# State-space stage of a hybrid decoder block: constant operand rows and the memory tokens' norm and splits made in the convolution stage and loaded; the exp table loaded behind attention

## The chip, the cores and the metric

One Trainium2 chip, of which one core runs this program. The core has a matrix engine (PE, with its weight loads listed apart as PEld), a vector engine (DVE), a scalar engine (ACT), a general engine (POOL) and a queue that issues DMA transfers (SP). The metric is the time of one execution on the device in microseconds; less is better.

## What is computed

One layer of a decoder trunk on 1024 tokens of width 1024, in three sub-layers, each with a norm before and after it and a residual. The change touches the first two:

```python
h = rms_norm(x, g_pre_mix)
q, k, v, z, xbc, dt_raw, ga, gs = split(h @ w_in)
o_att = stick_breaking_attention(q, k, v)                 # 16 heads of 64
o_ssm = ssd_branch(z, xbc, dt_raw, ...)                   # 32 heads in 4 groups, chunks of 128
merged = sigmoid(ga) * (o_att @ w_br_att) + sigmoid(gs) * (o_ssm @ w_br_ssm)
x = x + rms_norm(merged @ w_mix_out, g_post_mix)
h = rms_norm(x, g_pre_xa)
mem_n = rms_norm(mem, g_mem)                              # 256 memory tokens
x = x + rms_norm(memory_cross_attention(h, mem_n, w_xq, w_xkv, w_xo), g_post_xa)
...                                                       # dense SwiGLU
```

Inside `ssd_branch`, `x|B|C` go through a causal convolution of four taps and a SiLU. Then, for each chunk of 128 tokens, with `a_cs` the running sum of `dt * a` in the chunk:

```python
decay  = exp(where(tril, a_cs[l] - a_cs[s], -inf))        # per head, 128 x 128
y_diag = (C B^T * decay) (x dt)
states = B^T (decay_to_end * x dt)                        # passed from chunk to chunk
y_off  = exp(a_cs) * (C states_before)
```

## The kernel before

The program is one straight list of instructions without loops on the chip. A scheduler orders them at compile time, engine by engine: nearly as they are written, with later work moved up where it reckons an engine free and a buffer of the pool available. Buffers with one tag share a fixed number of slots. `behind(marks)` and `issue_behind` hold instructions behind a given one of the same engine. A float32 product is made as three products of split operands: `hi` is the rounded part, `lo` the rest (`hi_sb`, `lo_of`, `mm3`, L85 to L103).

Stages in order of time: the pre-norm; the token-major projections; the **convolution stage** (L476 to L615); **attention** (L625 to L828), with the last gates' projections (`gate_proj`, L711) between the heads; the **state-space stage** (L838 to L1180); the merge (L1197); cross-attention; the feed-forward layer.

*Convolution stage.* 18 pairs of 128 columns of `w_in` go through `pair` (L523): twelve with `conv`, six with `gate`. Each pair makes seven weight combinations on POOL (L198 to L201), splits them on ACT and DVE (L94, L97) into nine slots `sw`, multiplies (84 matmuls, L229 to L231), and adds up on DVE (L246 to L250). `conv` has three multiply-adds on DVE (L509), a sigmoid on ACT (L510) and a product on POOL (L511); its result is stored, or turned by PE transposes in `tail` (L499) during the next pair. Results and temporaries of 4 KB a partition share the six slots `b4`. Two small chains are set between the pairs: `dt_chain` (L540) ahead of the seventh, `dt_columns` (L587) ahead of the ninth.

*State-space stage.* The decay matrices come from a matmul (L937) of two operands whose rows hold a constant pattern and some rows of data: `colrows` (two buffers of 128 x 1024) gets rows of `sum_d` per chunk (L930), `keyrows` (two of 128 x 512) gets rows of `key_d` per four chunks (L894). The patterns are filled and selected on POOL (L874 to L879) and copied and completed on DVE (L882 to L886). All of the stage is then run over 32 chunks: `prep` two chunks ahead (loads, decay matmul, exp on ACT at L938, splits), `states`, `outp` (the matmuls `pd` at L989, the gated norm), and `flip` (four PE transposes of the chunk's output, L1011), which is called two chunks behind. `open_four` (L888) loads `bfm`, `cfm`, `btm` per four chunks; each of the three has a single buffer.

*Memory tokens.* `memory(m)` (L1058) loads 128 memory tokens, squares and norms them with the gain `gm`, turns them by eight PE transposes (L1067) and splits them into `mh`, `mlo` (L1069, L1070). It is called for both halves behind the first two `prep`. `mem_quanta` (L1072) then projects the tokens to keys and values in small pieces that are set between the first chunks' steps, and loads its own weights (L1083).

The exp table of ACT is loaded by the first exp of the stage, at L938; attention uses sigmoids (L714, L749) and copies.

The input `h` of the projections is held in eight tiles (b11, b21, b22, t1) on the left side of the memory up to the last gate projection. What the state-space stage allocates there takes their place; in order, these are the accumulators (L833), then `gbs`, `smp`, `s4p`, `s2p`, `exps`, `wr3`. The operand rows lie in `exps`.

## Time and profile before

| | |
|---|---|
| median of 3 runs | 2601.34 us (2600.95 to 2601.63) |
| the profiled execution's own time | 2600.91 us |
| its span in the trace | 2599.2 us |
| PE busy in the span | 2499.2 us (96%) |
| DVE busy | 1785.8 us (69%) |
| ACT busy | 1143.2 us (44%) |
| POOL busy | 864.8 us (33%) |
| convolution stage, first and last L229 on b11 | 287.7 to 627.5 us |
| attention's last matmul (L777) | 1109.8 us |
| decay matmuls (L937), first and last | 1117.7 to 1425.3 us |

Times are from one profiled execution and count from the start of its span. An engine's busy time says little by itself; what counts is which wait ends last at a given place. A view that lists stretches gives the busy time of each engine in each of them, and the TensorE clock that was granted, as a share of full speed.

### The profile page before, as it was taken

The page shows a single profiled execution, that of the slowest core. Times are in us where ns is not written, and L with a number is a line of the kernel's source. Part 1 is how long each engine was busy: PE and PEld are TensorE (multiplying, and loading weights), DVE is VectorE, ACT ScalarE, POOL GpSimd, SP SyncE. Part 2 cuts the span into 40 slices and gives each one's busy share as a digit, 9 for nine tenths or more (in the row PEclk, how much of TensorE's full clock was granted, in tenths as well). Part 3 has the DMA queues.
Part 4 walks back from the last instruction along what each step waited for, and adds up shares of the span by engine and source line. Part 5 has one row for each costly group of instructions (what it writes and reads, how often), then busy time and mean ns, then how long its engine had stood idle before and what let it go on. Part 6 is the DMA issues. An engine that isn't in the chain of part 4 may idle for free. (4 is left out here: it accounts for less than half of the span.)

```text
span 2599.2 us, 32676 instructions
## 1 busy us (share of the span) xinstructions
PE 2499.2 (96%) x12026; PEld 2072.4 (80%) x12026; DVE 1785.8 (69%) x2082; ACT 1143.2 (44%) x2037; POOL 864.8 (33%) x664
## 2 busy tenths in 40 slices
PE   5999999999999999989999999999999999999998
PEld 4888887788788888878888787887787888887876
DVE  7446778776477777588888665415459666665997
ACT  5333455555465665556544312314333333334343
POOL 5212544443211222235655150101114333323762
PEclk8999999999999999989999999999999999999999
DMA  5331343333534343356332472311232222234232
GB/s 176 111 108 57 122 130 101 106 113 114 154 98 110 92 124 93 91 177 196 107 95 71 142 251 84 119 61 49 81 118 73 78 90 81 77 93 170 98 130 98
DMA packets 250666, 288.50 MB, mean 111 GB/s; under 512 B 16767, under 2 KB 173064, under 8 KB 250122
## 3 DMA queue, kind: packets, MB, share of 16 engines
q1 hardware_dynamic: 250506, 286.41, 35.3%
q8 instruction: 95, 1.56, 0.2%
q14 instruction: 65, 0.53, 0.1%
HBM read 196.56 MB, written 73.01 MB: 104 GB/s over the span
## 5 line engine op out<-in xcount | busy, mean ns | idle before, releaser
L750 DVE TENSOR_TENSOR_SCAN n<-n,mask 128x128 f32<-128x128 f32 (+7 forms) x128 | 180.4, 1434 | 23.5 <-ACT n L749 22.2
L97 DVE TENSOR_TENSOR sw<-sf,sw 128x512 fp32r<-128x512 f32 x150 | 128.8, 871 | 67.5 <-ACT sw L94 67.2
L198 POOL TENSOR_TENSOR sf<-wr,wr 128x512 f32<-128x512 f32 x38 | 57.0, 1499 | 275.4 <-DMA wr<-in_w_in_dram 108.3
L767 ACT ACTIVATE wth<-tr,mone 128x512 fp32r<-128x512 f32 x192 | 109.9, 583 | 80.0 <-PE tr L764 79.3
L94 ACT ACTIVATE sw<-sf 128x512 fp32r<-128x512 f32 x150 | 92.0, 626 | 110.8 <-PE mm L231 95.1
L768 DVE SCALAR_TENSOR_TENSOR wtl<-tr,wth 128x512 fp32r<-128x512 f32 x192 | 99.4, 544 | 55.2 <-ACT wth L767 55.2
L94 ACT ACTIVATE sw<-wr 128x512 fp32r<-128x512 f32 x113 | 71.0, 629 | 127.2 <-PE mm L231 127.0
L231 PE MATMUL mm<-h,sw 128*128 128x512 f32 x320 | 124.8, 391 | 1.8 <-DVE sw L97 1.8
L100 PE MATMUL mm<-oth,bw 128*128 128x512 f32 (+1 forms) x320 | 122.3, 382 | 3.4 <-DVE a L1048 2.3
L229 PE MATMUL mm<-h,sw 128*128 128x512 f32 x320 | 122.6, 391 | 2.9 <-ACT h L94 2.3
L230 PE MATMUL mm<-h,sw 128*128 128x512 f32 x320 | 125.1, 391 | 0.0
L97 DVE TENSOR_TENSOR sw<-wr,sw 128x512 fp32r<-128x512 f32 x113 | 103.7, 918 | 24.8 <-ACT sw L94 16.9
L102 PE MATMUL mm<-oth,bw 128*128 128x512 f32 (+1 forms) x320 | 119.6, 374 | 0.6 <-DVE bw L97 0.6
L101 PE MATMUL mm<-otl,bw 128*128 128x512 f32 (+1 forms) x320 | 119.0, 372 | 0.0
L97 DVE TENSOR_TENSOR zl<-zr,zh 128x512 fp32r<-128x512 f32 x84 | 67.6, 810 | 72.3 <-ACT zh L94 72.1
L509 DVE SCALAR_TENSOR_TENSOR b<-b,prmT,b 128x1023 f32<-128x1023 f32 (+2 forms) x72 | 108.0, 1500 | 13.3 <-ACT b L507 12.7
L90 POOL TENSOR_SCALAR v<-va 128x512 fp32r<-128x512 f32 x16 | 20.6, 1288 | 277.3 <-PE av L777 164.6
L167 POOL TENSOR_SCALAR rstd<-ms 128x1 f32<-128x1 f32 x74 | 29.4, 397 | 238.8 <-ACT x L1269 113.0
L749 ACT ACTIVATE n<-sc 128x512 f32<-128x512 f32 (+1 forms) x192 | 88.6, 493 | 45.7 <-PE tr L764 28.9
L100 PE MATMUL p<-bw,h 128*128 128x512 f32 x256 | 99.6, 394 | 3.3 <-DVE x L1271 2.4
L94 ACT ACTIVATE zh<-zr 128x512 fp32r<-128x512 f32 x84 | 52.4, 630 | 113.8 <-PE mb L415 55.4
L102 PE MATMUL p<-bw,h 128*128 128x512 f32 x256 | 100.6, 394 | 0.0
(587 smaller groups left out, 8163.7 us busy)
## 6 DMA issues: line engine op xcount, KB each, us to landing
wr<-in_w_gu_dram SPq DMA_DIRECT2D x80, 256.0 KB
wr<-in_w_in_dram SPq DMA_DIRECT2D x36, 512.0 KB
zr<-in_w_in_dram SPq DMA_DIRECT2D x24, 512.0 KB
gu_d<-t SPq DMA_DIRECT2D x44, 256.0 KB
wraw<-in_w_in_dram SPq DMA_DIRECT2D x20, 512.0 KB
x<-in_x_dram SPq DMA_DIRECT2D x16, 512.0 KB
zs_d<-zo SPq DMA_DIRECT2D x32, 256.0 KB
xs_d<-b SPq DMA_DIRECT2D x32, 256.0 KB
```

The lines of the kernel that those rows point to most:

```text
L94: A.activation(o, i, AF.Copy)
L97: eng.tensor_tensor(o, i, hi.bitcast(F32), ALU.subtract)
L100: first = T.matmul(ps, sh, mh, start=start, stop=False)
L101: T.matmul(ps, sh, ml, start=False, stop=False)
L102: T.matmul(ps, sl, mh, start=False, stop=stop)
L229: T.matmul(ps, w[0][:, k, :], b[0][:, k, :], start=first and k == 0, stop=False, skip_group_check=True)
L230: T.matmul(ps, w[0][:, k, :], b[1][:, k, :], start=False, stop=False, skip_group_check=True)
L231: T.matmul(ps, w[1][:, k, :], b[0][:, k, :], start=False, stop=last and k == 3, skip_group_check=True)
L509: V.scalar_tensor_tensor(acc[:, sh:], y[:, :S - sh], cw(3 - sh, f), acc[:, sh:], ALU.mult, ALU.add)
L750: V.tensor_tensor_scan(nt[:, 0:L][:, ::-1], nt[:, 0:L][:, ::-1], mask[:, S - L:][:, ::-1], 1.0, ALU.mult, ALU.max)
L767: A.activation(wh[:, t0 * P:], pt[:, t0 * P:], AF.Identity, bias=mone)
L768: V.scalar_tensor_tensor(wl[:, t0 * P:], pt[:, t0 * P:], -1.0, wh[:, t0 * P:].bitcast(F32), ALU.add, ALU.subtract)
```

## The change

1. `patterns()`, called ahead of the second pair of the convolution stage, makes one copy of each operand-row pattern in slots `b4` and stores them to `colpat_d` and `keypat_d`. In the state-space stage, four loads fill the two `colrows` and the two `keyrows`. The pool `exps` is allocated first in its stage.
2. `memory()`, called ahead of the third pair, norms, turns and splits the memory tokens there, in slots `b4` and `b2` and the stage's own PSUM buffers, and stores the two parts to `mem_d`. In the state-space stage, four loads fill `mh` and `mlo`.
3. A one-column exp behind the last gate's sigmoid (`warm`).
4. The transposes of a chunk's `flip` are held behind the last `pd` matmul of the chunk two further on.
5. `FILL_LEFT`, an unused stretch of memory, shrinks by the 32 bytes that `warm` takes.

```diff
-FILL_LEFT, FILL_RIGHT = 128, 224
+FILL_LEFT, FILL_RIGHT = 96, 224
...
+    colpat_d = scr("colpat_d", [P, S])
+    keypat_d = scr("keypat_d", [P, HALF])
+    mem_d = [scr(f"mem_d{i}", [P, KT, ML]) for i in range(2)]
...
+            def patterns():
+                col, row, t = [mk(t4, [P, S], F32, "b4") for _ in range(3)]
+                before = t.rearrange("p (h s) -> p h s", s=P)
+                G.memset(before, 1.0)
+                G.affine_select(before, before, [[0, GH], [-1, P]], ALU.is_gt, 0.0, base=-2 * PAIRS, channel_multiplier=2)
+                V.tensor_copy(col.bitcast(F32R), t)
...
+                V.tensor_tensor(col[hr].rearrange("p (h s) -> p h s", s=P).bitcast(F32R), *heads, ALU.add)
+                nc.sync.dma_start(colpat_d, col)
+                within = row[:, HALF:].rearrange("p (c s) -> p c s", s=P)
+                G.memset(within, -(2.0 ** 120))
...
+                V.tensor_copy(row[:, 0:HALF].bitcast(F32R), row[:, HALF:])
+                V.tensor_scalar(row[ONES:ONES + 2, 0:HALF].bitcast(F32R), ident[ONES:ONES + 2, 0:1].to_broadcast([2, HALF]), 0.0, 1.0, ALU.mult, ALU.add)
+                nc.sync.dma_start(keypat_d, row[:, 0:HALF])
+
+            def memory():
+                gm, junk = [mk(t4, [P, D], F32, "b4") for _ in range(2)]
+                nc.sync.dma_start(gm, a["g_mem"][0].partition_broadcast(P))
+                for m in range(2):
+                    xt = mk(t4, [P, D], F32, "b4")
+                    nc.sync.dma_start(xt, a["mem"][0][m * P:(m + 1) * P, :])
+                    ms = mk(stats, [P, 1], F32, "ms")
+                    A.activation(junk, xt, AF.Square, scale=D ** -0.5, accum_out=ms)
+                    V.scalar_tensor_tensor(xt, xt, rstd_of(ms), gm, ALU.mult, ALU.mult)
+                    for kh in range(2):
+                        pt = mk(ps1, [P, HALF], F32, "tr")
+                        for k in range(4):
+                            T.transpose(pt[:, k * P:(k + 1) * P], xt[:, (kh * 4 + k) * P:(kh * 4 + k + 1) * P], ident)
+                        hi, lo = [mk(t2, [P, HALF], F32, "b2") for _ in range(2)]
+                        A.activation(hi.bitcast(F32R), pt, AF.Copy)
+                        V.tensor_tensor(lo.bitcast(F32R), pt, hi, ALU.subtract)
+                        for d, t in zip(mem_d, (hi, lo)):
+                            nc.sync.dma_start(d[:, kh * 4:kh * 4 + 4, m * P:(m + 1) * P], t.rearrange("p (k t) -> p k t", t=P))
+
             for i, j in enumerate(order):
+                if i == 1:
+                    patterns()
+                if i == 2:
+                    memory()
                 if i == 6:
                     dt_chain()
...
-                    A.activation(gt, ps, AF.Sigmoid)
+                    gated.append(A.activation(gt, ps, AF.Sigmoid))
...
+            with behind(gated[-1:]):
+                A.activation(warm, mone, AF.Exp)
...
+        ep = pool(p3, "exps", 1)
         gb = pool(p3, "gbs", 2)
         sm = pool(p3, "smp", 2)
         t4 = pool(p3, "s4p", 3)
         t2 = pool(p3, "s2p", 9)
-        ep = pool(p3, "exps", 1)
...
         for t in colrows:
-            V.tensor_copy(t, before)
-            V.tensor_tensor(t[hr], ...)
+            nc.sync.dma_start(t.rearrange("p h s -> p (h s)").bitcast(F32), colpat_d)
         for t in keyrows:
-            V.tensor_copy(t.rearrange("p (c s) -> p c s", s=P), within)
-            V.tensor_scalar(t[ONES:ONES + 2], ...)
+            nc.sync.dma_start(t.bitcast(F32), keypat_d)
...
-            for k in range(4):
-                T.transpose(pt[:, k, :], y[:, k * P:(k + 1) * P], ident)
+            with behind([chk[n + 2]["last"]] if n + 2 in chk else []):
+                for k in range(4):
+                    T.transpose(pt[:, k, :], y[:, k * P:(k + 1) * P], ident)
...
-        for m in range(2):
-            memory(m)
+        for kh in range(2):
+            for t, src in zip((mh, mlo), mem_d):
+                nc.sync.dma_start(t[:, kh * 4:kh * 4 + 4].bitcast(F32), src[:, kh * 4:kh * 4 + 4])
```

The old `memory(m)` and its tiles `gj`, `gm`, `junk_m` are gone from the state-space stage, as are the POOL fills and selects of L874 to L879.

More of the change, by code (lines that the diff above doesn't have):

```diff
@@ L155, in hybrid_block @@
     G.memset(mone, -1.0)
+    warm = mk(cp, [P, 1], F32, "warm")
     stats = pool(ctx, "stats", 16)
@@ L252, in winograd_pair @@
         return pa_
+    NROW, HEADS, ONES, PAIRS, LARGE = 2, 32, 0, 64, 2.0 ** 127
     HB = ("b11", "b21", "b22", "t1")
@@ L709, in qk_proj @@
                 return dense(C_Q + hp * P, ev_q), dense(C_K + hp * P, ev_k)
+            gated = []
             def gate_proj(gi):
@@ L859, in hybrid_block @@
         four = {}
-        NROW, HEADS, ONES, PAIRS, LARGE = 2, 32, 0, 64, 2.0 ** 127
         low = mk(ep, [P, P], F32, "low")
@@ L872, in hybrid_block @@
         keyrows = [mk(ep, [P, HALF], F32R, f"keyrows{i}") for i in range(2)]
-        before, within = mk(t4, [P, GH, P], F32, "s4"), mk(t4, [P, GH, P], F32, "s4")
-        G.memset(before, 1.0)
-        G.affine_select(before, before, [[0, GH], [-1, P]], ALU.is_gt, 0.0, base=-2 * PAIRS, channel_multiplier=2)
-        within = within[:, 0:4]
-        G.memset(within, -(2.0 ** 120))
-        G.affine_select(within, within, [[0, 4], [1, P]], ALU.is_ge, 0.0, base=2 * PAIRS, channel_multiplier=-2)
-        G.affine_select(within, within, [[0, 4], [-1, P]], ALU.is_ge, 0.0, base=1 - 2 * PAIRS, channel_multiplier=2)
-        hr = slice(HEADS, HEADS + 2 * GH)
         for t in colrows:
-            V.tensor_copy(t, before)
-            V.tensor_tensor(t[hr], *[ident[hr, HEADS + j * GH:HEADS + (j + 1) * GH].unsqueeze(2).to_broadcast([2 * GH, GH, P]) for j in range(2)], ALU.add)
+            nc.sync.dma_start(t.rearrange("p h s -> p (h s)").bitcast(F32), colpat_d)
         for t in keyrows:
-            V.tensor_copy(t.rearrange("p (c s) -> p c s", s=P), within)
-            V.tensor_scalar(t[ONES:ONES + 2], low[ONES:ONES + 2, 0:1].to_broadcast([2, HALF]), 0.0, 1.0, ALU.mult, ALU.add)
+            nc.sync.dma_start(t.bitcast(F32), keypat_d)
         def open_four(g, q):
@@ L991, in outp @@
                     marks.append(ins)
+            d["last"] = ins
             V.tensor_tensor(y, y, pd, ALU.add)
@@ L1052, in hybrid_block @@
         mlo = mk(ot, [P, KT, ML], F32R, "otl")
-        gj = mk(wp, [P, 4, D], F32, "bw")
-        gm, junk_m = gj[:, 0], gj[:, 1]
-        nc.sync.dma_start(gm, a["g_mem"][0].partition_broadcast(P))
         marks = []
-        def memory(m):
-            xt = mk(wr, [P, D], F32, "wraw")
-            nc.sync.dma_start(xt, a["mem"][0][m * P:(m + 1) * P, :])
-            ms = mk(stats, [P, 1], F32, "ms")
-            A.activation(junk_m, xt, AF.Square, scale=D ** -0.5, accum_out=ms)
-            V.scalar_tensor_tensor(xt, xt, rstd_of(ms), gm, ALU.mult, ALU.mult)
-            for kh in range(2):
-                pt = mk(ps, [P, 4, P], F32, "mm", bufs=2)
-                for k in range(4):
-                    T.transpose(pt[:, k, :], xt[:, (kh * 4 + k) * P:(kh * 4 + k + 1) * P], ident)
-                ks, cs = slice(kh * 4, kh * 4 + 4), slice(m * P, (m + 1) * P)
-                A.activation(mh[:, ks, cs], pt, AF.Copy)
-                V.tensor_tensor(mlo[:, ks, cs], pt, mh[:, ks, cs].bitcast(F32), ALU.subtract)
         def mem_quanta():
```

4 lines of the change are left out of this document (added).

## Prediction

> **What bounds the kernel now.** I began with the page: the profiled execution has a span of 2599.2 us, 1.7 us less than its own time of 2600.91 us, and PE is busy nearly everywhere in it.
>
> ```profile
> span 2599.2 us, 32676 instructions
> ```
>
> The change touches two places only: the convolution stage (L476 to L615) and the seam at which attention ends and the state-space stage begins. So I next read the table of stretches around the seam (columns: stretch, its length, then busy us and instructions of PE, PEld, DVE, ACT, POOL, then the granted clock, the DMA share and GB/s).
>
> ```profile
> 1100.00:1110.00 10.00, 7.45 (x41) 5.22 (x39) 5.39 (x11) 5.63 (x11) 1.48 (x3) 1.00 0.56 150
> 1110.00:1120.00 10.00, 6.28 (x19) 3.85 (x18) 9.17 (x15) 6.67 (x11) 2.99 (x4) 0.52 0.68 207
> 1120.00:1130.00 10.00, 9.91 (x50) 8.24 (x50) 10.00 (x9) 8.45 (x16) 7.70 (x6) 0.80 0.72 216
> 1130.00:1140.00 10.00, 6.94 (x29) 4.79 (x29) 10.00 (x13) 5.43 (x9) 2.09 (x3) 0.71 0.50 145
> 1140.00:1150.00 10.00, 10.00 (x65) 9.81 (x66) 8.26 (x11) 4.17 (x9) 5.51 (x7) 0.78 0.44 130
> ```
>
> Two losses of PE are to be seen. It is idle for 2.55 + 3.72 + 0.09 + 3.06 = 9.4 us, and what it does run from 1110 on runs at a lowered clock: busy time times the missing share gives 6.28 x 0.48 + 9.91 x 0.20 + 6.94 x 0.29 + 10.00 x 0.22 = 9.2 us (an estimate, since the clock is a mean of its stretch). Together 18.6 us are lost here. DVE is busy 9.17 + 10.00 + 10.00 = 29.2 of the 30 us from 1110 to 1140, so between these points it is DVE that PE waits for, directly or through a chain.
>
> The timeline of the seam shows what stands in these queues (start, us, engine, line, operation; in brackets the idle time before it and its releaser).
>
> ```profile
> 1102.16 0.60 ACT L714 ACTIVATE gt<-mm 128x512 f32<-128x512 f32 x1 [0.24 <-PE mm L102]
> 1102.31 0.42 SPq L898 DMA_DIRECT2D cfm<-cf_d  x1
> 1103.26 6.68 SPq L900 DMA_DIRECT2D btm<-bt_d  x2
> ...
> 1106.79 0.63 ACT L94 ACTIVATE ch<-cfm 128x512 fp32r<-128x512 f32 x1 [2.37 <-DMA cfm<-cf_d]
> ...
> 1107.94 0.44 PE L776 MATMUL av<-wth,v 128*128 128x384 f32 x1 [2.07 <-ACT wth L767]
> ...
> 1109.66 1.28 DVE L882 CAST colrows<-s 128x1024 fp32r<-128x1024 f32 x2
> 1110.86 0.76 DVE L885 CAST keyrows<-s 128x512 fp32r<-128x512 f32 x2
> 1111.65 2.35 DVE L883 TENSOR_TENSOR colrows<-ident 16x1024 fp32r<-16x1024 f32 x2
> 1113.09 4.30 SPq L930 DMA_DIRECT2D colrows<-sum_d  x4
> 1115.82 0.41 DVE L886 TENSOR_SCALAR keyrows<-low 2x512 fp32r<-2x512 f32 x1
> ...
> 1117.65 1.19 PE L937 MATMUL dec<-colrows,keyrows 128*128 128x512 f32 x2 [1.37 <-DMA colrows<-sum_d]
> 1117.96 1.28 ACT L938 ACT_TABLE_LOAD   x1
> ```
>
> The chain to the first decay matrix is: last attention step, constants on DVE, the rows of `sum_d` written into them, matmul at 1117.65, exp table, exp. A different wait comes earlier: ACT stands 2.37 us for `cfm` with the last attention copies behind it in its queue, and PE's 2.07 us before L776 come from that.
>
> **The change, part by part.** *Constants.* From DVE's seam go 1.28 + 0.76 + 2.35 + 2 x 0.41 = 5.2 us. In their place stand four loads, 2 x 512 KB + 2 x 256 KB. Their tiles move to the front of the pool, so to addresses which the projections' input h held; they come free when the last gate projection is done, about 1102, not behind the last attention step. The `sum_d` and `key_d` rows now wait for these loads, where they waited for DVE. Behind them on SP stand the `btm`, `xs` and memory loads. The other bound on this is SP itself: for 6.68 us from 1103.26 it is held by the second `btm`, which waits for its only buffer, so `sum_d` may still not go out before about 1110, 3 us earlier than now.
>
> *Memory tokens.* The norm, the transposes and the splits leave the seam.
>
> ```profile
> L1063 DVE SCALAR_TENSOR_TENSOR wraw<-wraw,rstd,bw x2: 1693/1874/2056, 1119.4 to 1126.3; 128x1024 f32<-128x1024 f32 x2
> L1070 DVE TENSOR_TENSOR otl<-mm,oth x4: 674/676/677, 1129.9 to 1140.4; 128x512 fp32r<-128x512 f32 x4
> 1123.12 1.46 PE L1067 MATMUL mm<-ident,wraw 128*128 128x128 f32 x8
> 1130.63 1.25 PE L1067 MATMUL mm<-ident,wraw 128*128 128x128 f32 x8 [0.72 <-DVE otl L1070]
> 1610.24 1.03 PE L180 MATMUL tr<-ident,x 128*128 128x128 f32 x8
> ```
>
> That is 2 x 1.87 + 4 x 0.68 = 6.5 us of DVE, and 2.7 us of PE, which at full clock would be 2 x 1.03 = 2.1 us (eight such transposes at L180). With the constants DVE loses 11.7 of its 29.2 us in the bound stretch. The split tokens come back as four loads of 512 KB in place of the gain and the two token loads of 512 KB each, and their first user, the memory projection, which started only behind L1070's last at 1140.4, can fill PE's hole at 1130 to 1140.
>
> *DMA at the seam.* 1.5 MB of constants and 2 MB of tokens come, 1.5 MB go: 2.0 MB more, on five more issues. From 1100 to 1130 the rows move 1.50 + 2.07 + 2.16 = 5.7 MB; 7.8 MB would need 27 us at the 293 GB/s of the next row (PE, clock, DMA share, GB/s). They fit, but not by much, and if they don't, 1.5 MB cost 5.4 us.
>
> ```profile
> 640.00:645.00 5.00, 5.00 (x24) 1.00 0.96 293
> ```
>
> *Exp table.* The load of 1.28 us goes from between the first decay matmul and its exp to behind the last gate's sigmoid, which ran at 1102.16. There the 2.37 us that ACT stands before `ch` cover it; without that cover it would delay the last attention copies by 1.3 us. The Trainium skill ("ScalarE: Activation LUTs", What ACT_TABLE_LOAD costs) counts about 2.66 us for a switch, a drain included; by that the term would be 2.7 us and not 1.3. The row shows 1.28 us alone, the exps following at once, so the sum goes by 1.3.
>
> *Seam, summed.* Of the 9.4 us of idle time I keep the tail of attention (2.55, its cause `cfm` is untouched) and half of 3.72, as `sum_d` gains 3 us at best and the table 1.3; the hole of 3.06 I take as filled but for 0.5. That gives 1.9 + 2.5 = 4.4. Of the clock's 9.2 I keep half, 4.6, as the first gap stays and with it the first lowering. The transposes give 2.1 at full clock. Sum 11.1; I take **10 us**, since DVE can also be late with what it has left. Lower bound 3 us (only `sum_d`'s lead, everything else waiting for loads), upper 17 (all but the tail's idle time and two clock us).
>
> *Convolution stage.* All of it is added there: POOL work, one set of constants on DVE (half of 5.2), the memory tokens' 6.5, so 9.1 us of DVE, ACT's squares and copies, 16 transposes, some 4.3 MB on 13 issues of SP.
>
> ```profile
> 290.00:310.00 20.00, 19.25 (x85) 15.58 (x84) 15.73 (x18) 9.57 (x16) 11.99 (x9) 1.00 0.53 158
> 310.00:330.00 20.00, 20.00 (x94) 16.64 (x93) 18.84 (x16) 10.21 (x17) 11.76 (x8) 1.00 0.30 92
> 330.00:350.00 20.00, 20.00 (x94) 16.64 (x93) 13.41 (x14) 11.37 (x17) 9.36 (x6) 1.00 0.46 153
> 350.00:370.00 20.00, 20.00 (x94) 16.66 (x93) 14.51 (x13) 10.01 (x16) 10.03 (x6) 1.00 0.38 112
> ...
> 430.00:450.00 20.00, 16.06 (x66) 12.11 (x64) 19.79 (x27) 8.03 (x10) 8.97 (x6) 0.91 0.19 56
> 450.00:470.00 20.00, 18.87 (x87) 15.43 (x88) 13.95 (x22) 12.46 (x21) 6.27 (x4) 1.00 0.53 158
> ```
>
> PE is full there, so the transposes cost their 2.1 us in any case. DVE's 9.1 us meet 4.3 + 1.2 + 6.6 + 5.5 = 17.6 us of idle time in 80, ACT has half its time free, and 4.3 MB fit beside 92 to 158 GB/s. So stalls can be zero. The other bound is the place where such work was already put in, `dt_chain` (L540): from 430 to 470 DVE fills up to 19.79 of 20, and PE loses 3.94 + 1.13 of idle time and 16.06 x 0.09 = 1.4 of clock, 6.5 us. With DVE at 18.84 (310 to 330) PE still lost nothing, so I take a value in the lower half, 2 us. **Cost 4 us**, bounds 2 and 9.
>
> The squares need no table of their own there: in the last stage, too, squares (L1698) run behind sigmoids (L1436) without a load between them.
>
> *Order of the flips.* Holding a flip's transposes behind the last `pd` matmul two chunks on is what PE does anyway, chunk for chunk, so I cost it at nothing (at most 0.6 us each in the first chunks).
>
> ```profile
> 1310.30 1.89 PE L989 MATMUL pd<-s,s 128*128 128x96 f32 x16
> 1314.86 0.60 PE L1011 MATMUL ptr<-ident,s 128*128 128x128 f32 x4
> ```
>
> **Sum.** 2600.9 - 10 + 4 = 2594.9; the profiled execution is 0.4 us under the median of 2601.34, so 2595 is the time either way. A measurement of this kernel can tell about 0.2%, 5.2 us, from no change.
>
> **Rivals.** *Loads take DVE's place*: SP's queue holds the constants' rows up to 1110 and the tokens land no sooner than the projection began. The seam then gives its lower bound, 3 to 5, the stage takes 4: 2601. For it speaks the 6.68 us row; against it that DVE's 29.2 of 30 us lose 11.7 whatever SP does.
>
> *The convolution stage takes it back*: stalls as at `dt_chain`, 6.5, with 2.1 of transposes, 8.6 in all, and 10 at the seam: 2599. What would make it so are POOL's new fills and selects, as DVE slows beside POOL:
>
> ```profile
> 310.18 2.27 POOL L201 TENSOR_TENSOR sf<-wr,sf 128x512 f32<-128x512 f32 x1
> 311.23 1.78 DVE L97 TENSOR_TENSOR sw<-sf,sw 128x512 fp32r<-128x512 f32 x1
> 316.42 0.68 DVE L97 TENSOR_TENSOR sw<-sf,sw 128x512 fp32r<-128x512 f32 x1
> ```
>
> The same subtraction takes 0.68 us alone and 1.78 beside L201. The Trainium skill says as much ("GPSIMD Engine Reference", 1. Specifications): the SBUF interfaces are shared, with contention for DVE instructions of two SBUF inputs. The trace agrees, by 1.1 us in this pair.
>
> *Slower*: the constants' 1.5 MB go out ahead of `cfm`. Then `cfm` lands 5.4 us later, ACT holds the last attention copies behind `ch`, and the whole seam shifts by that; it decides itself by SP's order at 1102 and by ACT keeping `ch` ahead of L767. Of the 10 us then 10 - 5.4 - 1.9 (the tail's gap, 2.07, more than doubled, brings an earlier clock loss) = 3 are left, and with stalls of 9 in a stage that gets its weights through the same SP queue behind the tokens' stores: +6, 2607.
>
> *More*: the projection fills all of PE's holes, the clock stays up: 16 at the seam, 3 in the stage, 2588.
>
> *It doesn't do what it says*: a sigmoid scheduled behind the early table load would bring the load back at 1.28 us, in the seam: part of the first rival.
>
> **Chances.** Forecast 0.42 (own range 2591 to 2598; three quarters of it beyond 5.2 us), more 0.15, loads 0.15, convolution 0.13, slower 0.15. Faster by over 0.2%: 0.33 + 0.15 = 0.48; within: 0.09 + 0.15 + 0.13 = 0.37; slower 0.15. The range of 8 in 10 is 2586 to 2606: it leaves out the better part of "more" and half of "slower".
>
> **What would show it.** DVE from 1110 to 1140 well under 29 us; the first L937 at about 1113 to 1115, no table load before its exp; the memory projection's first matmuls before 1135; PE's clock above 0.9 after 1130; in the stage PE full from 290 to 370 but for 4 us, its end (last L231 there) 4 us later than now. I am wrong if `cfm`, the constants or the tokens release PE at the seam, or if PE shows gaps of 2 us and a lowered clock before 400.

## The result: 17.9 us slower, and the profile after

The changed kernel took 2619.34 us (median of 4 runs, 2618.66 to 2623.62), the kernel before, run beside it, 2601.49 us (2600.95 to 2603.95). The ratio is 1.0068, with a 95% interval of 1.0055 to 1.0081: slower by 0.7%, where 0.2% can be told from no change. The forecast was 2595 us.

The profiled execution of the changed kernel took 2618.99 us. Its page begins so:

```profile
span 2617.2 us, 32721 instructions
```

Three groups of matmuls cut the span into stages: the scores (`sc`, attention), `av` (their product with the values) and `pd` (the output of each chunk of the state-space stage). The view of a tile's instructions gives each group's first start and last end (columns: line, engine, operation, count; ns min, median, max; first and last start or end in us; forms). First the kernel before:

```profile
L747 PE MATMUL sc<-kh,qs x192: 218/389/504, 691.8 to 1088.5; 128*128 128x512 f32 x96, 128*128 128x128 f32 x32, 128*128 128x256 f32 x32, 128*128 128x384 f32 x32
L748 PE MATMUL sc<-kl,qs x192: 220/364/479, 692.9 to 1088.8; 128*128 128x512 f32 x96, 128*128 128x128 f32 x32, 128*128 128x256 f32 x32, 128*128 128x384 f32 x32
L989 PE MATMUL pd<-s,s x512: 243/275/421, 1124.9 to 1448.2; 128*128 128x96 f32 x149, 128*128 128x64 f32 x22
```

Then the changed kernel:

```profile
L804 PE MATMUL sc<-kh,qs x192: 218/389/501, 705.8 to 1105.4; 128*128 128x512 f32 x96, 128*128 128x128 f32 x32, 128*128 128x256 f32 x32, 128*128 128x384 f32 x32
L805 PE MATMUL sc<-kl,qs x192: 223/364/475, 707.0 to 1105.6; 128*128 128x512 f32 x96, 128*128 128x128 f32 x32, 128*128 128x256 f32 x32, 128*128 128x384 f32 x32
L1032 PE MATMUL pd<-s,s x512: 242/275/423, 1135.3 to 1465.0; 128*128 128x96 f32 x149, 128*128 128x64 f32 x22
```

| stretch | before | after | difference |
|---|---|---|---|
| start to first `sc` (convolution stage and what lies ahead of it) | 691.8 | 705.8 | +14.0 |
| first to last `sc` (attention) | 397.0 | 399.8 | +2.8 |
| last `sc` to last `pd` (seam and state-space stage) | 359.4 | 359.4 | 0.0 |
| last `pd` to the end | 1151.0 | 1152.2 | +1.2 |
| span | 2599.2 | 2617.2 | +18.0 |

So the seam, forecast to give 10 us, gave nothing, and the convolution stage, forecast to cost 4, cost 14. The last line is within what that stretch, which the change doesn't touch, differs by among the kernels below (1149 to 1156 us). The 2.8 us of attention stay unexplained: the kernels with an edit in the convolution stage have 397.6 to 400.4 there, those without 397.0 to 398.9.

**The seam.** The table of stretches of the changed kernel, 16 us later than the rows of the prediction, since attention ends 15.6 us later (columns as there):

```profile
1116.00:1126.00 10.00, 8.39 (x46) 6.11 (x43) 4.64 (x8) 6.85 (x13) 0.50 (x2) 1.00 0.70 221
1126.00:1136.00 10.00, 7.33 (x20) 4.84 (x21) 5.17 (x7) 5.69 (x10) 1.28 (x2) 0.57 0.90 284
1136.00:1146.00 10.00, 9.14 (x48) 8.19 (x48) 6.47 (x6) 4.31 (x8) 4.62 (x4) 0.75 0.83 274
1146.00:1156.00 10.00, 10.00 (x79) 9.60 (x80) 10.00 (x11) 4.97 (x9) 4.34 (x3) 1.00 0.92 279
1156.00:1166.00 10.00, 8.84 (x66) 8.18 (x65) 8.44 (x9) 7.04 (x13) 8.50 (x8) 1.00 0.90 269
```

DVE was busy 29.2 of 30 us there and is busy 5.17 + 6.47 + 10.00 = 21.6 now: that relief came. What took its place is the DMA: 0.83 to 0.92 busy for 40 us at 269 to 284 GB/s, where before it was 0.44 to 0.72. The timeline just behind attention's last matmul:

```profile
1125.40 0.33 PE L834 MATMUL av<-wtl,v 128*128 128x128 f32 x1
...
1127.85 2.04 PE L955 MATMUL dec<-cfm,bfm 128*128 128x128 f32 x8 [2.11 <-DMA cfm<-cf_d]
...
1129.88 2.24 PE L980 MATMUL dec<-colrows,keyrows 128*128 128x512 f32 x3
...
1131.06 1.04 POOL L987 TENSOR_TENSOR s<-s,wm 128x512 f32<-128x512 f32 x1 [11.45 <-DMA s<-xs_d]
```

The first decay matmul comes 4.5 us behind the last `av`, not 7.9. But PE now waits for `cfm`, and POOL's product of `xs` and `wm` (L987) waits for the load of `xs`. In the kernel before, POOL had done that work ahead of attention's end at 1109.8 (POOL's timeline):

```profile
1089.27 0.95 POOL L874 MEMSET s<- 128x1024 f32 x1 [22.56 <-PE sc L748]
...
1093.57 1.04 POOL L944 TENSOR_TENSOR s<-s,wm 128x512 f32<-128x512 f32 x1
1094.57 0.63 POOL L879 TENSOR_SCALAR_AFFINE_SELECT s<-s 128x512 f32<-128x512 f32 x1
1095.17 2.49 POOL L944 TENSOR_TENSOR s<-s,wm 128x512 f32<-128x512 f32 x2
1097.63 1.49 POOL L978 TENSOR_TENSOR s<-s,dsk 128x512 f32<-128x512 f32 x1
```

The constants are gone from there, as meant, but so are four products of L944 (the fourth at 1100.01) and one of L978: `exps` stands first among the pools now, the tiles of `xs` lie behind it, and come free with attention's last tiles. (That this place is the reason is tested in e8, below.)

In these five rows the loss of PE (the stretch less busy time times clock) falls from the 18.6 us of the prediction to 1.6 + 2.7 + 0.9 + 0 + 1.2 = 6.3 of idle time and 7.33 x 0.43 + 9.14 x 0.25 = 5.4 of clock, 11.7 in all: 6.9 less.

How much of the relief stayed? Two rows per kernel, cut at the last `av` matmul: its first 60 us and the next 80. Before:

```profile
1109.80:1169.80 60.00, 52.50 (x318) 45.78 (x319) 50.88 (x58) 36.06 (x62) 24.22 (x24) 0.80 0.59 180
1169.80:1249.80 80.00, 77.31 (x422) 65.25 (x421) 64.16 (x72) 46.99 (x86) 42.84 (x38) 1.00 0.55 176
```

After:

```profile
1125.40:1185.40 60.00, 53.36 (x332) 46.73 (x332) 47.91 (x48) 33.88 (x59) 31.94 (x24) 0.89 0.78 244
1185.40:1265.40 80.00, 73.15 (x382) 60.25 (x381) 65.14 (x73) 45.20 (x83) 43.70 (x39) 0.98 0.50 165
```

In the first 60 us the loss falls from 60 - 52.50 x 0.80 = 18.0 to 60 - 53.36 x 0.89 = 12.5, a gain of 5.5. In the next 80 it rises from 80 - 77.31 = 2.7 to 80 - 73.15 x 0.98 = 8.3, 5.6 back. The counts of PE say the same: 332 instructions in place of 318, then 382 in place of 422.

**The convolution stage.** The answers to the prediction's rows:

```profile
310.00:330.00 20.00, 20.00 (x94) 16.44 (x93) 17.88 (x13) 9.14 (x15) 15.17 (x12) 1.00 0.24 79
330.00:350.00 20.00, 16.11 (x70) 12.78 (x69) 13.73 (x16) 9.05 (x15) 7.71 (x6) 0.89 0.73 250
350.00:370.00 20.00, 20.00 (x92) 16.48 (x91) 12.35 (x16) 9.94 (x18) 4.99 (x5) 0.94 0.56 171
370.00:390.00 20.00, 18.91 (x90) 14.99 (x88) 17.61 (x14) 9.45 (x15) 12.95 (x6) 1.00 0.45 144
390.00:410.00 20.00, 18.15 (x79) 14.85 (x80) 17.12 (x18) 11.78 (x19) 10.55 (x6) 1.00 0.42 146
...
450.00:470.00 20.00, 13.53 (x60) 10.13 (x59) 19.83 (x27) 9.11 (x15) 7.06 (x4) 1.00 0.14 40
```

From 330 to 350 DVE (13.73 of 20) and ACT (9.05) are far from full, and still PE loses 3.9 us of idle time and 16.11 x 0.11 = 1.8 of clock. The timeline shows why:

```profile
343.31 0.39 PE L236 MATMUL mm<-t1h,sw 128*128 128x512 f32 x1
...
345.90 1.06 ACT L642 ACTIVATE b<-b 128x1024 f32<-128x1024 f32 x1 [6.09 <-DMA b<-in_mem_dram]
...
346.95 0.58 ACT L244 ACTIVATE b<-mm 128x512 f32<-128x512 f32 x1
...
347.58 0.80 PE L234 MATMUL mm<-t2h,sw 128*128 128x512 f32 x1 [3.89 <-ACT b L244]
```

The square of the memory tokens (L642) stands at the head of ACT's queue for 6.09 us, until its load has landed. Behind it stands the copy L244 that empties a PSUM bank, and PE waits for that bank. A little later the eight stores of the split tokens stand in SP's queue:

```profile
351.98 3.26 SPq L200 DMA_DIRECT2D wr<-in_w_in_dram  x2
356.09 13.89 SPq L652 DMA_DIRECT2D mem_d<-b  x8
379.32 0.37 SPq L200 DMA_DIRECT2D wr<-in_w_in_dram  x1
```

With the two tiles of `b2` the stores run one behind the other, to 369.98, and ACT stands 3.53 us (at 359.59) and 1.94 us (at 362.65) for a tile that is still being stored. PE is full from 350 to 380 all the same. The next weights go out at 379.32, where before they went at 367.49, but the stores are not what holds them: SP stands free for 9.3 us behind the last store, until DVE's split (L101) has freed the weights' tile. A second loss, 2.9 us of idle time, comes from 380 to 395. Its longest wait, 2.18 us at 391.85, is for DVE's sum L253, which empties a bank and stands behind two multiply-adds of the convolution:

```profile
386.59 4.61 DVE L521 SCALAR_TENSOR_TENSOR b<-b,prmT,b 128x1023 f32<-128x1023 f32 x2 [0.77 <-ACT b L519]
```

They take 4.61 us here, beside POOL's L203 and L204; two such took 2.59 us at 366.39, with POOL idle. Summed over stretches of 20 us from 270 to the first score matmul, idle time and clock cost PE 15.0 us before and 25.3 after, 10.4 of the 14.0; 2.1 more are the transposes, and 1.5 are not accounted for.

### The profile page after: what moved, and what is told of

The parts are those of the page before. It is cut to its first block, busy times and chain, and to the rows that moved or that the text cites. A ratio compares the mean times of both kernels' runs of the same rounds, so it can differ in the third digit from the quotient of the medians.

```text
span 2617.2 us, 32721 instructions
## 1 busy us (share of the span) xinstructions
PE 2503.8 (96%) x12026; PEld 2072.5 (79%) x12026; DVE 1796.4 (69%) x2078; ACT 1142.1 (44%) x2038; POOL 867.3 (33%) x664
## 5 line engine op out<-in xcount | busy, mean ns | idle before, releaser
L807 DVE TENSOR_TENSOR_SCAN n<-n,mask 128x128 f32<-128x128 f32 (+7 forms) x128 | 186.1, 1479 | 24.1 <-ACT n L806 20.8
L101 DVE TENSOR_TENSOR sw<-sf,sw 128x512 fp32r<-128x512 f32 x150 | 128.5, 870 | 65.5 <-ACT sw L98 65.3
L203 POOL TENSOR_TENSOR sf<-wr,wr 128x512 f32<-128x512 f32 x38 | 57.3, 1508 | 277.3 <-DMA wr<-in_w_gu_dram 105.3
L521 DVE SCALAR_TENSOR_TENSOR b<-b,prmT,b 128x1023 f32<-128x1023 f32 (+2 forms) x72 | 112.3, 1559 | 12.6 <-ACT b L519 12.0
L101 DVE TENSOR_TENSOR sw<-wr,sw 128x512 fp32r<-128x512 f32 x113 | 103.3, 916 | 22.3 <-ACT sw L98 22.0
L101 DVE TENSOR_TENSOR zl<-zr,zh 128x512 fp32r<-128x512 f32 x84 | 67.6, 811 | 72.2 <-ACT zh L98 72.0
```

What stands on the lines that cost most here:

```text
L101: eng.tensor_tensor(o, i, hi.bitcast(F32), ALU.subtract)
L521: V.scalar_tensor_tensor(acc[:, sh:], y[:, :S - sh], cw(3 - sh, f), acc[:, sh:], ALU.mult, ALU.add)
L807: V.tensor_tensor_scan(nt[:, 0:L][:, ::-1], nt[:, 0:L][:, ::-1], mask[:, S - L:][:, ::-1], 1.0, ALU.mult, ALU.max)
```

## The experiments

All were timed beside the kernel before. "Stage" is the first score matmul against before's 691.8, "seam on" the time from the last `sc` to the last `pd` (before 359.4), both from the one profiled execution, whose own time can lie several us from its kernel's median (e4: 2617.08 us against 2625.94).

| run | ratio to before, 95% | stage | seam on |
|---|---|---|---|
| the whole change | 1.0068 [1.0055, 1.0081] | +14.0 | 359.4 |
| e1: constants, `exps` first | 1.0014 [1.0002, 1.0025] | +1.8 | 360.8 |
| e2: memory tokens | 1.0024 [1.0011, 1.0037] | +6.0 | 362.1 |
| e3: early exp | 0.9999 [0.9987, 1.0012] | 0.0 | 360.6 |
| e16: held flips | 1.0003 [0.9990, 1.0017] | -0.2 | 358.8 |
| e8: `exps` first, alone | 1.0036 [1.0022, 1.0049] | -0.4 | 369.1 |
| e10: constants, `exps` last | 1.0012 [1.0000, 1.0024] | +2.2 | 358.7 |
| e11: constants, `s2p` first | 1.0040 [1.0026, 1.0055] | +3.2 | 368.1 |
| e4: whole, `exps` last | 1.0080 [1.0054, 1.0107] | +11.0 | 364.1 |
| e6: whole, no token loads at the seam | 1.0090 [1.0073, 1.0107] | +14.2 | 361.5 |
| e15: whole, projection over 10 chunks | 1.0074 [1.0051, 1.0096] | +15.5 | 363.3 |
| e5: whole, memory tokens two pairs later | 1.0081 [1.0066, 1.0096] | +11.6 | 365.3 |
| e7: whole, squares behind their pair | 1.0097 [1.0081, 1.0112] | +18.6 | 360.1 |
| e9: whole, loads a pair ahead | 1.0082 [1.0065, 1.0099] | +20.9 | 362.3 |
| e12: e9 with `s2p` first | 1.0063 [1.0047, 1.0079] | +16.2 | 359.4 |
| e13: whole, loads without work | 1.0042 [1.0029, 1.0054] | +8.8 | 361.3 |
| e14: whole, work without loads | 1.0057 [1.0042, 1.0072] | +14.9 | 358.4 |

The change, e4, e6 and e15 have the same convolution stage and show +11.0 to +15.5: differences below about 4 us in that column tell nothing. e5, e7 and e9 have the same seam as the whole change and show 360.1 to 365.3 us for its 359.4: differences below about 6 us in the last column tell nothing either. None of the kernels beats the one before.

### The parts by themselves

e1 takes `patterns()`, the four loads and the place of `exps`; e2 `memory()`, its stores and loads; e3 `warm` and `FILL_LEFT`.

```diff
+                if i == 1:
+                    patterns()
...
+            nc.sync.dma_start(t.rearrange("p h s -> p (h s)").bitcast(F32), colpat_d)
```

> Only the constants' part of the change: patterns() in the convolution stage, four loads at the seam, the pool of the operand rows first. Memory tokens, exp table and flips as before. Theory A (the memory tokens' norm in the convolution stage does the harm, since its square waits for its load in ACT's queue ahead of copies that PE needs): first scores 1 to 3 us later than before (693 to 695, before 691.8), time 2599 to 2604. Theory B (POOL's fills and selects and the DVE copies do it): first scores 6 us or more later, time 2606 or more.

```diff
+                if i == 2:
+                    memory()
...
+                nc.sync.dma_start(t[:, kh * 4:kh * 4 + 4].bitcast(F32), src[:, kh * 4:kh * 4 + 4])
```

> Only the memory tokens' part: norm, transposes and splits in the convolution stage, four loads at the seam. Constants, exp table and flips as before. Theory A: first scores 9 to 13 us later than before (701 to 705), PE idle 3 to 4 us behind an ACT square that waits for the token load; the seam gives back 2 to 4, time 2608 to 2612. Theory B: first scores 3 to 6 us later, time 2602 to 2605.

```diff
+            with behind(gated[-1:]):
+                A.activation(warm, mone, AF.Exp)
```

> Only the early exp behind the last gate's sigmoid. If the 2.4 us that ACT stands before ch cover it: 2599.5 to 2601 (0 to 1.3 us faster, no table load before the first decay exp). Rival: it delays the last attention copies, as in the changed kernel, where the load ran at 1119.6 and the next copy only at 1121.0: 2602 to 2603, attention's last matmul 1 to 1.5 us later.

None of them gains at the seam: 360.8, 362.1 and 360.6 us against 359.4. In the stage the constants cost 1.8 and the memory tokens 6.0, of which 2.1 are transposes. The two sum to 7.8, while the whole change shows 11 to 15.5: they are dearer together. Part of the reason is in the traces. The first tokens' load goes out at 338.30 in the whole change, straight behind the constants' stores on SP (332.49 and 335.20); in e2 it goes out 14 us earlier:

```profile
338.30 0.63 SPq L640 DMA_DIRECT2D b<-in_mem_dram  x1
```

```profile
323.99 0.33 SPq L610 DMA_DIRECT2D b<-in_mem_dram  x1
...
342.87 1.06 ACT L612 ACTIVATE b<-b 128x1024 f32<-128x1024 f32 x1 [4.04 <-DMA b<-in_mem_dram]
```

So e2's first square runs at 332.09 without waiting for its load. The second, shown, waits 4.04 us for its own, and PE stays full through it:

```profile
330.00:350.00 20.00, 20.00 (x99) 16.70 (x98) 13.23 (x13) 12.10 (x23) 10.07 (x9) 1.00 0.53 166
```

A waiting square is thus not dear by itself; what counts is whether PE runs out of emptied banks before the copy behind it. The early exp gives and takes nothing.

The held flips alone:

```diff
+            with behind([chk[n + 2]["last"]] if n + 2 in chk else []):
```

> The kernel before with one edit: the transposes of a flip wait for the last pd matmul two chunks on. The prediction costs this at nothing, since PE's order is that already. If so, last score matmul to last pd stays at 358 to 361 us (before 359.4) and the time is within 0.1% of before. If the wait holds ACT's and DVE's copies of the flips back and with them the branch projection: 362 us or more and 2605 or more.

Nothing is to be seen of them either, as was expected.

### The seam: place of the pools, loads, projection

```diff
+        ep = pool(p3, "exps", 1)
         gb = pool(p3, "gbs", 2)
...
-        ep = pool(p3, "exps", 1)
```

> The kernel before with nothing changed but the place of the operand rows' pool: first in its stage. If that place is what takes the preparation (xs loads, POOL products, splits) from ahead of attention's end: POOL's busy time in the 20 us before attention's last matmul falls from 10.8 to under 6, and the first chunk's products come 10 us or more later; the constants' DVE work moves ahead of attention's end by 5 us. Time 2601 to 2606. Rival (the place is harmless): 2597 to 2600, as DVE's 5.2 us leave the seam.

This edit changes no instruction, only the place of tiles, and the stretch from the seam on is 9.7 us longer; the ratio of 1.0036, about 9 us, bears that out. In the 10 us ahead of the last `av` matmul (here 1113.6) PE falls to 5.71, where before it had 7.45:

```profile
1094.00:1104.00 10.00, 10.00 (x57) 8.49 (x56) 3.22 (x7) 4.49 (x9) 1.98 (x5) 1.00 0.36 103
1104.00:1114.00 10.00, 5.71 (x27) 4.09 (x25) 8.83 (x16) 4.20 (x8) 0.25 (x1) 0.77 0.43 132
```

The constants' tiles come free early, so DVE makes the constants (8.83 of 10 us busy) between attention's last steps, and PE waits 4.3 us in all for DVE's part of those (L768). POOL's preparation hardly runs (1.98 and 0.25 us): its first product of `xs` starts only at 1119.92, behind 15.67 us of idle time that the load of `xs` ended. So the place of the pool alone costs 9.7 us, and loading the constants gives 8.3 of it back (e8 to e1).

The other way round, `exps` last in the whole change, and in the constants alone:

```diff
-        ep = pool(p3, "exps", 1)
         gb = pool(p3, "gbs", 2)
...
+        ep = pool(p3, "exps", 1)
         wr = pool(p3, "wr3", 3)
```

> The whole change, but the pool of the operand rows allocated last in its stage, as before the change. If the pool's place is what eats the seam's gain (the token rows xs land 30 us later than before, since their buffers then share memory with attention's last tiles): xs loads and POOL's products return to about 15 us ahead of attention's end, PE's idle time behind the first decay matmul shrinks, 2613 to 2616. Rival (the constants' loads need the early place): they start only behind attention's end, the first decay matmul 3 us or more later than 12.2 us after the last gate matmul, 2619 to 2624.

> The constants made in the convolution stage and loaded, as in e1, but with the exps pool last, as in before: the xs and zs loads then go out 10 to 30 us ahead of attention's end again, the constants' loads behind them. Theory (the place of the pool costs 9.7 us, as in e8, and loads instead of DVE's work are worth 8.3): with the pool at its old place the two add up, last score matmul to last pd is 351 to 354 us, and the time is 2596 to 2598. Rival (with the pool last the constants' tiles come free only with attention's last ones, so the 1.5 MB land on the path that DVE's 5.2 us stood on): 359 to 364 us, and the time is 2601 to 2608.

The two effects don't add up to a gain: 364.1 and 358.7 us. In e10 the table of stretches from the last `av` (1114.4) on shows the new limit:

```profile
1114.40:1124.40 10.00, 8.24 (x25) 5.28 (x25) 6.42 (x9) 4.53 (x8) 5.59 (x4) 0.66 0.79 269
1124.40:1134.40 10.00, 6.33 (x35) 4.25 (x34) 6.63 (x7) 9.41 (x17) 5.80 (x7) 1.00 0.78 256
```

DVE has 3.4 to 3.6 us free in each, and PE isn't full for it; the first decay matmul of e10 comes 11.6 us behind the last `av` (before 7.9), as the constants' tiles come free late and 1.5 MB have to land.

Placing `s2p` ahead of `exps` was to have both early:

```diff
+        t2 = pool(p3, "s2p", 9)
         ep = pool(p3, "exps", 1)
```

> As e1 (constants loaded), with the order of the pools s2p, exps, gbs, smp, s4p: the tiles of xs and zs and the constants' tiles both stand at addresses that come free early, and the tiles of cfm, btm and seg come later. Theory (the gain is kept when both the early loads of xs and the constants run ahead of attention's end): the first xs load is issued before 1090 and the constants before 1110, last score matmul to last pd is 351 to 356 us, the time 2596 to 2600. Rival (something must stand last, and bfm, cfm and btm are then what the first decay matmul waits for): 359 us or more, the time 2602 or more.

It gave 368.1 us, in an execution of 2618.71 us against a median of 2612.74. But the order didn't do what it was meant to: the first load of `xs` went out at 1108.83, behind the constants' at 1105.72, and not before 1090. What having both early would be worth stays untested. Together with the memory tokens' part (e12, below) the same order gave 359.4.

Next the 2 MB of loads, which are left out in e6 (POOL fills the split tokens with 0.01 instead, so their values are not the reference's):

```diff
-                nc.sync.dma_start(t[:, kh * 4:kh * 4 + 4].bitcast(F32), src[:, kh * 4:kh * 4 + 4])
+                G.memset(t[:, kh * 4:kh * 4 + 4].bitcast(F32), 0.01)
```

> The whole change, but the four loads of the memory tokens' parts at the seam are left out (POOL fills the tiles with a constant, so the memory tokens' values are not the reference's). If the 2 MB hold the seam up: the 40 us behind attention's last matmul show a DMA share under 0.8 where the change has 0.86 to 0.92, and the last decay matmul comes 4 us or more earlier against attention's last matmul than in the change (316.8). Rival (what was done ahead of attention's end, and isn't any more, holds it up): no more than 1.5 us.

361.5 us: without these 2 MB it is no shorter. The DMA is still 0.87 busy in the 20 us behind the last `av`, but these bytes are not what sets the end of the stage. Last, the projection spread wider, so that it fills PE for longer:

```diff
-        MEM_SPAN = 8
+        MEM_SPAN = 10
```

> The whole change with the memory projection spread over 10 chunks instead of 8 (MEM_SPAN). In the changed kernel PE loses 13.7 us from the last score matmul to 60 us behind the last av matmul, 6.3 less than before, but 8.4 us in the 80 us after that, 5.7 more. Theory (the projection, started earlier, runs out as filler for the chunks' waits): spread wider it leaves more to fill, the loss in those 80 us falls to 4 us or less, and last score matmul to last pd falls from 359.4 to 356 us or less. Rival (the chunks' own chains on ACT and DVE set the pace once the seam is past, whatever fills PE): 358 to 362 us, and the loss only moves.

The rival held: 363.3 us, no gain, with the projection's last products 109 us behind the last `av` and not 91 as in the change. The loss in the 80 us behind the first 60 was 80 - 73.91 x 0.96 = 9.0, not 4:

```profile
1186.10:1266.10 80.00, 73.91 (x381) 61.84 (x382) 61.26 (x72) 44.76 (x82) 44.15 (x39) 0.96 0.51 166
```

### The convolution stage: place, loads, work

```diff
-                if i == 2:
+                if i == 4:
                     memory()
```

> The whole change, but memory() called ahead of the fifth pair of the convolution stage (a gate pair), not the third. Theory A2 (constants alone cost the stage 1.8 us, memory tokens alone 6.0, together 14.0, since the token load queues behind the constants' stores and ACT's square stands for it ahead of copies that PE needs): apart from the constants the two add up, first scores 7 to 9 us later than before (699 to 701), 2610 to 2613. Rival (sheer amount of DVE and POOL work, wherever it is put): first scores 12 to 15 us later, 2617 to 2620.

Two pairs away from the constants the stage still loses 11.6 us, not the 7.8 of the parts apart. The wait is another one: ACT's squares are late here too, and then DVE's norm takes 3.46 us beside POOL's L523 instead of 1.28, with the transposes waiting for it:

```profile
391.79 3.46 DVE L643 SCALAR_TENSOR_TENSOR b<-b,rstd,b 128x1024 f32<-128x1024 f32 x1 [1.52 <-POOL rstd L173]
...
395.39 1.94 PE L647 MATMUL tr<-ident,b 128*128 128x128 f32 x8 [9.24 <-DVE b L643]
```

The next two give the loads a lead. In e7 the gain and the first token tile are loaded at the old place and the rest stands behind that pair; the second load is then late in its turn. In e9 all three loads stand one pair ahead.

```diff
+                    if m == 0:
+                        yield
+                        junk = mk(t4, [P, D], F32, "b4")
...
+                    rest = memory()
+                    next(rest)
...
+                if i == 2:
+                    for _ in rest:
+                        pass
```

> The whole change, but of memory() only the loads of the gain and of the first 128 tokens are set ahead of the third pair; the squares, transposes, splits and stores stand behind that pair's work. Theory A2: no PE wait of 3 to 4 us with ACT behind a square, PE's clock stays at 1.00 to 370, first scores 6 to 10 us later than before (698 to 702). Rival (stores through two slots and late weight loads do it): first scores still 12 us or more later.

```diff
-                gm, junk = [mk(t4, [P, D], F32, "b4") for _ in range(2)]
+                gm, *xts = [mk(t4, [P, D], F32, "b4") for _ in range(3)]
...
+                yield
+                junk = mk(t4, [P, D], F32, "b4")
...
+                if i == 3:
+                    for _ in rest:
+                        pass
```

> The whole change, with the gain and both token tiles loaded one pair of blocks ahead of their norm (three b4 tiles held for one pair longer), the scratch tile of the squares taken only with the norm. In the changed kernel ACT stands 6.1 us at the first square for the token load, with the copies behind it for which PE waits; in the run with only the first token load ahead (e7) ACT stood 4.2 us at the second square instead, and PE lost 7.1 us. Theory (a square in ACT's in-order queue that waits for its own load is what makes the stage dear): no square waits over 0.5 us for a load, no idle time of PE over 2 us behind L244's copy between 330 and 400, and the first score matmul comes 4 to 8 us behind before's 691.8 (1.8 for the constants, 2.1 for the transposes, the rest for DVE and the stores) instead of 11 to 14. Rival (the tiles of the b4 pool, or the engines' time, are what is short): still 11 us or more. In both the seam and the state-space stage stay at 359 to 362 us.

Both are worse, +18.6 and +20.9. In e9 no square waits for a load any more, as was meant; it waits for its tile:

```profile
371.56 1.06 ACT L522 ACTIVATE b<-b 128x1024 f32<-128x1024 f32 x1 [2.65 <-DVE b L521]
375.12 1.06 ACT L644 ACTIVATE b<-b 128x1024 f32<-128x1024 f32 x1 [2.50 <-POOL b L523]
...
377.48 0.60 ACT L244 ACTIVATE b<-mm 128x512 f32<-128x512 f32 x1
```

```profile
378.13 0.79 PE L234 MATMUL mm<-t2h,sw 128*128 128x512 f32 x1 [9.89 <-ACT b L244]
```

The squares' scratch tile is one of the six of `b4`. Three are held by the loads, the next one is free only when the convolution of the pair before has gone through DVE, ACT and POOL (L521 to L523), and PE stands 9.89 us behind that chain. Whether a seventh tile would help was not tried.

> The whole change with the loads ahead of the norm (as e9) and the pools in the order s2p, exps, gbs, smp, s4p (as e11). If both theories hold: convolution stage 4 to 8 us dearer than before, seam and state-space stage 350 to 355 us against 359.4, in all 2596 to 2604. If the rivals hold: 2615 or more.

e12 has both edits of e9 and e11. The stage's part of the theory fell with e9, and the seam stayed at 359.4: the rivals held, 2619.48 us.

e13 keeps the tiles and the loads, and leaves out norm, transposes, splits and stores; e14 keeps the work and fills the tiles by POOL (in both the memory tokens' values are not the reference's, as in e6).

```diff
-                    V.scalar_tensor_tensor(xt, xt, rstd_of(ms), gm, ALU.mult, ALU.mult)
-                    for kh in range(2):
...
+                    A.activation(junk[:, 0:1], xt[:, 0:1], AF.Square, scale=D ** -0.5, accum_out=ms)
+                    V.tensor_tensor(xt[:, 0:1], xt[:, 0:1], gm[:, 0:1], ALU.mult)
```

> The whole change, but of the memory tokens' part in the convolution stage only the tiles, the three loads of 512 KB, and a square and a product of one column each are kept: norm, transposes, splits and stores are left out, and the split tokens are filled with 0.01 at the seam (so the memory tokens' values are not the reference's). It is compared with e6, which fills them too and has the whole part: its first score matmul came 14.2 us behind before's. Theory (what is dear is the wait of ACT and SP for the loads and for free b4 tiles, not the work): the first score matmul is still 9 us or more behind before's 691.8. Rival (it is the work: 6.5 us of DVE, ACT's copies, 2.1 us of transposes, the stores that hold SP): 5 us or less, near the 1.8 of the constants alone.

```diff
-                nc.sync.dma_start(gm, a["g_mem"][0].partition_broadcast(P))
+                G.memset(gm, 1.0)
...
-                    nc.sync.dma_start(xt, a["mem"][0][m * P:(m + 1) * P, :])
+                    G.memset(xt, 0.01)
```

> The whole change, but the gain and the token tiles in the convolution stage are filled by POOL instead of loaded (gain 1, tokens 0.01), and the split tokens are filled at the seam as in e6 (so the memory tokens' values are not the reference's). Everything else of the part stays: the four b4 tiles, squares, norm, transposes, splits and stores. Compared with e6, 14.2 us behind before at the first score matmul. If the loads (their waits on ACT and SP, and their 1.5 MB beside the weights) are what is dear: 7 us or less behind 691.8. If the work and the tiles are: 9 us or more. In e13 and e14 together the shares of loads and work can be read; if both come out small, it is their meeting that costs.

With the loads and no work the stage is at +8.8, between the two cases; 1.8 of it are the constants'. The work without the loads cost no less than the whole, 14.9 against 14.2 in e6. In e13 ACT stood just as long as in the changed kernel:

```profile
345.96 0.20 ACT L642 ACTIVATE b<-b 128x1 f32<-128x1 f32 x1 [6.10 <-DMA b<-in_mem_dram]
```

and in e14 it stood for what came in the loads' place, POOL's fills, and then for the stores:

```profile
340.42 1.06 ACT L642 ACTIVATE b<-b 128x1024 f32<-128x1024 f32 x1 [3.87 <-POOL b L640]
358.17 0.60 ACT L649 ACTIVATE b<-tr 128x512 fp32r<-128x512 f32 x1 [4.52 <-DMA mem_d<-b]
```

The loss of PE, summed by 20 us as above, tells the two apart, since the added work stands between 270 and 410 us:

| kernel | 270 to 410 | 410 to 650 | 650 to first `sc` |
|---|---|---|---|
| before | 1.1 | 9.8 | 4.0 |
| e1: constants | 1.8 | 9.4 | 4.9 |
| e2: memory tokens | 4.2 | 9.7 | 4.5 |
| the whole change | 10.9 | 9.6 | 4.9 |
| e13: loads without work | 4.8 | 9.5 | 8.3 |
| e14: work without loads | 11.1 | 9.2 | 7.1 |

Where the tokens' part stands, the loads by themselves cost 3 us more than the constants alone, and the work by itself, its tiles filled by POOL, as much as the whole. Half of e13's +8.8 lies behind 650, which its edit doesn't touch. So a load is not needed for the cost; work that has to wait for something at the head of a queue is enough (3.87 us for POOL's fills in e14).

## Why the prediction was wrong

**What bounds the seam: right, but only for 60 us.** DVE was what PE waited for there, DVE did lose a good quarter of its work (7.6 of 29.2 us, where 11.7 were forecast), no table load stood before the first decay exp any more, and the loss of PE in the first 60 us fell by 5.5 us, within the bounds of 3 to 17. The memory projection began at 1135.0 (before 1141.0), 9.6 us behind the last `av` instead of 31.2. In the stretch that the prediction summed up, to 40 us behind the last `av`, its terms nearly came about: 3.1 us of idle time gained for a forecast 4.4, 3.8 of clock for 4.6.

**The step that failed at the seam is the sum: idle time removed at the seam was taken as time removed from the span.** The prediction's sum ends at 1150. The 5.5 us come back in the 80 us behind, in the changed kernel and, with 7.9 to 8.5 us lost in that stretch against 2.7 (summed by 20 us), in e2, e4, e6, e9 and e12, which all have the memory tokens' part; e1, e8, e10 and e11, without it, lose 2.7 to 6.1. From the last `sc` to the last `pd` it is 359.4 us either way. Spreading the filler (e15) doesn't help. What PE waits for there are above all the chunks' own exps on ACT (3.4 us) and products on DVE (1.7). That these are the pace of the stage is the reading that fits; no run here takes one of them away, so it isn't shown.

**A term was left out: the place of the pool.** The prediction read `exps` first as good for the constants and didn't ask which tiles moved back in its place. e8 prices that at 9.7 us, as large as the whole forecast gain, and e1 shows that the loaded constants just make up for it. A price of e8 may not be taken off the change's result, though: e4, with the old place, is no faster.

**The clock** was to stay above 0.9 behind 1130, which is 20 us behind attention's end. Counted from there it did: 0.57 and 0.75 in the first 20 us and 1.00 from 1146 on, where before it was still 0.78. PE's first gap stayed, now for `cfm` (2.11 us), and the lowered clock followed it. So the signs that the prediction named for the seam came about (the first decay matmul, the projection, DVE, the clock), and with them the sign of being wrong, `cfm` releasing PE; signs within 40 us of the seam could not tell that the span would not follow.

**Rivals at the seam.** "Loads take DVE's place" was nearest: the DMA went to 0.83 to 0.92 busy and `cfm` and `xs` are waited for. But its mechanism (SP held by the second `btm`) didn't come about, its gain of 3 to 5 was too high, and in e6 the seam is no shorter without the tokens' bytes.

**The convolution stage: a term of 4 us, bounds 2 to 9, that measured 14.0 (11.0 to 15.5 in four kernels).** The transposes' 2.1 us were about right (2.2: 1.04 for eight and twice 0.60 for four, at 354.83, 361.16 and 365.06). The step that failed is "stalls can be zero", where the free time of DVE and ACT in 80 us was set against the work added. The work did fit: from 330 to 350 DVE and ACT have 6.3 and 11 us free. What isn't free is the place in the order: the square at the head of ACT's queue for 6.09 us costs PE 3.89 us of idle time and about 3 of clock behind it (1.8 in the stretch to 350 and 1.2 in the next), and two multiply-adds ahead of L253 in DVE's queue 2.18 us more; with other orders it is the norm (e5) or the six tiles of `b4` (e9). The prediction weighed only the DVE-filled stretch of `dt_chain` as an upper bound, and this is another mechanism. The sign by which it would be wrong was named: gaps of 2 us and a lowered clock before 400. Rival "the convolution stage takes it back" had the wrong price (8.6), and its cause, DVE slowed beside POOL, is a smaller part: 4.61 us for 2.59 ahead of the 2.18 us wait, and 3.46 us for 1.28 in e5. What slowed DVE there were the stage's own POOL products, not the constants' fills that the rival named. The Trainium skill ("GPSIMD Engine Reference", 1. Specifications) names a contention of DVE instructions of two SBUF inputs with POOL for their shared interfaces, and the row of e5 agrees with that.

**"Slower"** had the right sign and stalls of 9 us, but behind the tokens' stores on SP, to which no wait of PE is traced; at the seam it had another cause, and 2607 was 12 us short. Why the two parts cost 7.8 us apart and 11 to 15.5 together is answered in part: behind the constants' stores the first load goes out 14 us later than in e2. It stays open beyond that, since e5 loses as much two pairs away, at another wait, and e14 without any load.

**Exp table and flips: right in size, empty in effect.** e3 and e16 are within 0.1% of before. The early table load took 1.28 us again, the exp behind it following at once:

```profile
1119.63 1.28 ACT L888 ACT_TABLE_LOAD   x1
...
1120.92 0.20 ACT L888 ACTIVATE warm<-mone 128x1 f32<-128x1 f32 x1
```

The Trainium skill's 2.66 us ("ScalarE: Activation LUTs", What ACT_TABLE_LOAD costs) are not seen here, and by neither figure would the result come out another way.

## What to carry to other kernels

Free time of an engine says that moved work fits, not that it is free: ask what it stands ahead of in each in-order queue (a square waiting 6 us for its load held the copy that PE waited for, where one waiting 4 us in e2 cost PE nothing), and which ring of tiles it takes from. Where a loss is removed at a seam, look 100 us further on before it goes into the sum: here 5.5 us were gained in 60 and 5.6 lost in the next 80. Name signs for that stretch too, or the signs can all come true beside a slower kernel. And a change of the order of pools is an edit of its own, to be priced by itself: it decides which loads can run ahead of the stage.

## What was not expected of the hardware

A load of 512 KB is not a fixed time: the first tokens' load, issued at 338.30, released its square at 345.90, 7.6 us later, with 250 GB/s moving in that stretch; in e2, without the constants' stores ahead of it, the second tokens' load was issued at 338.58 and released its square at 342.87, 4.3 us later, with 166 GB/s in the same stretch. And a gap can cost PE more than its length: behind the 3.89 us at 347.58 the matmuls take 0.63 us instead of 0.39 until 352.4, which makes up most of the 0.89 and 0.94 in the clock column; the 3.0 us for which PE waited at the same place in e13 left that column at 1.00.
